# Strassen's method for the up projections of a two-layer decoder trunk

## The chip, the cores and the metric

The kernel runs on one core of one Trainium2 chip. The metric is the time on the device of one execution, in microseconds (us). TensorE (PE in the profile, with PEld for its weight loads) does the matrix products and writes to PSUM; VectorE (DVE), ScalarE (ACT) and GpSimd (POOL) do the elementwise work; the SyncE queue (SP) starts the transfers.

## The reference

The reference is one inference step of a trunk with two layers, for a prompt of 512 tokens and for 8 samples of 8 tokens. The kernel treats these as one matrix of T = 576 tokens. Layer 0 mixes the tokens by attention and a recurrent branch, layer 1 by causal pooling, and each layer ends in a gated network with a short convolution in time:

```python
def _conv_ffn(xn, prev, w_up, cw, cb, w_down):
    u = jnp.einsum("btd,df->btf", xn, w_up)          # 1024 -> 6144
    uc, new_prev = _causal_dwconv(u, prev, cw, cb)   # three taps in time
    g, val = jnp.split(uc, 2, axis=-1)               # 3072 each
    return jnp.einsum("btf,fd->btd", jax.nn.gelu(g) * val, w_down), new_prev
# in _trunk, for each layer, after the mixer:
xn = _rmsnorm(x, p["norm_ffn"][layer])
y, fb = _conv_ffn(xn, ffn_buf[layer], p["ffn_w_up"][layer], ...)
x = x + y
```

Everything is float32. The change touches the two calls of `_conv_ffn` alone.

## The kernel before

The residual lies transposed in `xT`: eight chunks of 128 channels (on partitions) by 576 tokens. Products are made in three parts: each float32 operand is split into a rounded part and a remainder, and rounded times rounded, rounded times remainder and remainder times rounded are added in PSUM. `split` (L115) makes the two parts of 128 weight columns by 1024 rows (tile `whl`): ACT rounds and DVE subtracts. `mm3` (L126) makes one block of 128 output channels: for each of K chunks of the contraction three weight blocks, each used for both halves of the tokens (HT = 288 columns), so 6K matmuls into two PSUM banks.

A gated network is `ffn` (L1216). Its input is `xgh`, `xgl`: the two parts of x times the gain, not yet divided by the root mean square. The division comes after the product. `rstd` (L233) works out the factor while the first products run and spreads it over partitions in `rb`, and the evacuation of every up product multiplies by `rb`. `up_pair(i)` (L1244) makes column block i of the gate half and of the value half. Each is 48 matmuls in `mm3`, three evacuations (L1268 to L1270) into `u`, three taps of the convolution (L1277 on ACT, L1278 and L1279 on DVE, with small copies of state on POOL); then follow the gelu, the product of the halves (L1284, L1285), and its split into `hh`, `hl` (L1288, L1289). After each eight blocks `down(p)` (L1301) multiplies by 1024 rows of the down weights: eight output chunks of 48 matmuls, each added to `xT` by `add_x` (L703). The weights come by transfers of 1 MB for two column blocks (`raw`, L109).

There are 24 blocks, so one gated network has 24 x 96 = 2304 matmuls up and 24 x 48 = 1152 down. PSUM is one pool of eight banks. Small work (`states`, `tails`) hangs in the queue `bg` and is put in by `tick` between products. The order on each engine is the scheduler's of the language, which keeps near to the order of the program; a queue is run in that order.

## Time and profile before

| | us |
|---|---|
| median of three runs | 1289.35 (1287.3 to 1292.38) |
| the profiled execution | 1290.56 |
| its span in the trace | 1288.8 |
| PE busy | 1272.3 (99%) |
| DVE busy | 816.6 (63%) |
| ACT busy | 536.3 (42%) |
| POOL busy | 167.6 (13%) |

The profiled execution is 1.8 us longer than its span and 0.1% above the median. Busy time of PE counts a matmul until its modelled end, so a busy PE says that it never stood empty, not that it was at its peak; the rate is read from the chain of work, which gives so many matmuls in so many us.

### The profile page before, as it was taken

How to read it: one execution, taken by the hardware profiler on the slowest of the kernel's cores; microseconds unless marked ns; L12 is line 12 of the kernel's file. 1: busy time of each engine (PE TensorE's matmuls, PEld its weight loads, DVE VectorE, ACT ScalarE, POOL GpSimd, SP SyncE). 2: the span in 40 equal slices, each digit the busy share in tenths (PEclk: the TensorE clock that was granted, in tenths of full speed). 3: DMA queues.
4: the chain of work that ended last, by engine and by line, in shares of the span. 5: the costliest groups of instructions: out<-in, count | busy, mean ns of one | idle time of the engine just before them, and what ended most of it. 6: DMA issues, size and time to landing. Idle time of an engine off the chain costs nothing.

```text
span 1288.8 us, 22949 instructions
## 1 busy us (share of the span) xinstructions
PE 1272.3 (99%) x9422; PEld 1221.3 (95%) x9422; DVE 816.6 (63%) x1571; ACT 536.3 (42%) x889; POOL 167.6 (13%) x530
## 2 busy tenths in 40 slices
PE   8999989999999999999999999999999999999998
PEld 6988878889999999999999999899999999999998
DVE  6847979887767436664376658766643767346742
ACT  6656567764434213432234336443412343124331
POOL 2240064282100000000000003210000000000000
PEclk9999999999999999999999999999999999999999
DMA  6223343342322232222322112422232232233131
GB/s 167 97 68 102 100 138 89 90 161 69 103 68 76 68 117 81 68 68 86 113 66 65 62 36 74 149 71 67 68 100 99 67 101 68 67 99 100 35 96 47
DMA packets 105918, 111.64 MB, mean 87 GB/s; under 512 B 6722, under 2 KB 96970, under 8 KB 105805
## 3 DMA queue, kind: packets, MB, share of 16 engines
q1 hardware_dynamic: 101668, 101.68, 24.5%
q0 software_dynamic: 3072, 8.46, 2.4%
q8 instruction: 74, 1.21, 0.4%
q14 instruction: 32, 0.25, 0.1%
q10 hardware_dynamic: 1072, 0.04, 0.1%
HBM read 104.14 MB, written 6.25 MB: 86 GB/s over the span
## 4 chain that ended last, share of the span: by engine, by line
PE 78%; DVE 5%; ACT 1%; issue 1%; ACTq 0%
PE mmb L135 73%; PE mmb L903 1%; PE mmb L691 1%; PE mmb L866 1%; DVE whl L123 1%; DVE xl L285 0%; PE mmb L920 0%; ACT zh L1149 0%; DVE eb L836 0%; PE mmb L849 0%; DVE st L833 0%; DVE xT L1179 0%; PE mmb L1232 0%; DVE zl L1150 0%; DVE pl L853 0%
## 5 line engine op out<-in xcount | busy, mean ns | idle before, releaser
L135 PE MATMUL mmb<-xh,whl 128*128 128x288 f32 x3456 | 613.8, 298 | 0.0
L135 PEld LDWEIGHTS mmb<-xh,whl 128*128 128x128 f32 x3456 | 512.2, 189 | 2.7 <-ACT kT L649 0.2
L135 PE MATMUL mmb<-xl,whl 128*128 128x288 f32 x1728 | 371.6, 296 | 1.6 <-DVE xl L285 1.6
L122 ACT CAST whl<-wraw 128x1024 fp32r<-128x1024 f32 (+1 forms) x172 | 178.7, 1040 | 365.2 <-PE mmb L135 261.3
L135 PEld LDWEIGHTS mmb<-xl,whl 128*128 128x128 f32 x1728 | 279.2, 189 | 2.2 <-DVE xl L285 2.1
L135 PE MATMUL mmb<-hh,whl 128*128 128x288 f32 x1536 | 269.8, 295 | 0.1
L123 DVE TENSOR_TENSOR whl<-wraw,whl 128x1024 fp32r<-128x1024 f32 (+1 forms) x172 | 209.8, 1220 | 84.2 <-ACT whl L122 83.9
L135 PEld LDWEIGHTS mmb<-hh,whl 128*128 128x128 f32 x1536 | 225.7, 188 | 0.7 <-ACT hh L1288 0.6
L135 PE MATMUL mmb<-hl,whl 128*128 128x288 f32 x768 | 164.8, 295 | 0.0
L703 DVE TENSOR_TENSOR xT<-mmb,xT 128x288 f32<-128x288 f32 x112 | 46.1, 452 | 146.6 <-PE mmb L135 146.3
L1268 DVE TENSOR_TENSOR u<-mmb,rb 128x288 f32<-128x288 f32 x96 | 44.0, 458 | 134.2 <-PE mmb L135 127.5
L1273 POOL COPY ut<-u 128x18 f32<-128x18 f32 x96 | 23.1, 241 | 777.7 <-DVE u L1270 777.7
L135 PEld LDWEIGHTS mmb<-hl,whl 128*128 128x128 f32 x768 | 122.9, 188 | 0.0
L1288 ACT CAST hh<-hf 128x576 fp32r<-128x576 f32 x48 | 32.4, 674 | 139.0 <-DVE hf L1285 139.0
L1277 ACT ACTIVATE t<-u,par 128x592 f32<-128x592 f32 x96 | 84.7, 882 | 3.6 <-POOL u L1272 2.0
L1279 DVE SCALAR_TENSOR_TENSOR t<-u,par,t 128x592 f32<-128x592 f32 x96 | 80.2, 835 | 3.4
L1278 DVE SCALAR_TENSOR_TENSOR t<-u,par,t 128x592 f32<-128x592 f32 x96 | 79.5, 828 | 1.1 <-ACT t L1277 1.0
L1282 ACT ACTIVATE t<-t 128x592 f32<-128x592 f32 x48 | 33.6, 700 | 94.9 <-DVE t L1279 94.9
L1289 DVE TENSOR_TENSOR hl<-hf,hh 128x576 fp32r<-128x576 f32 x48 | 36.4, 758 | 34.8 <-ACT hh L1288 34.8
L580 PE MATMUL mmb<-whl,xh 128*128 128x512 f32 x192 | 53.2, 394 | 0.0
L580 PEld LDWEIGHTS mmb<-whl,xh 128*128 128x128 f32 x192 | 35.3, 188 | 8.1 <-ACT a__257 L1462 0.4
L1269 DVE TENSOR_TENSOR u<-mmb,rb 128x224 f32<-128x224 f32 x96 | 36.5, 380 | 0.0
(394 smaller groups left out, 1321.7 us busy)
## 6 DMA issues: line engine op xcount, KB each, us to landing
wraw<-in_ffn_w_up SPq DMA_DIRECT2D x48, 1024.0 KB
wraw<-in_ffn_w_down SPq DMA_DIRECT2D x24, 1024.0 KB
wraw<-in_ab_w_in SPq DMA_DIRECT2D x9, 1024.0 KB
wraw<-in_ab_w_out SPq DMA_DIRECT2D x4, 1024.0 KB
xt<-in_x_prompt SPq DMA_DIRECT2D x4, 512.0 KB
out_y_p<-y SPq DMA_DIRECT2D x8, 256.0 KB
wraw<-in_ab_w_in SPq DMA_DIRECT2D x2, 512.0 KB
out_k_p<-X SPq DMA_DIRECT2D x1, 1024.0 KB
```

The source lines that it names most:

```text
L122: keep(self.nc.scalar.copy(hi, v))
L123: keep(self.nc.vector.tensor_tensor(lo, v, hi.bitcast(F32), SUB))
L135: nc.tensor.matmul(ps[hf][:, 0:HT], w[:, k, :], x[:, hf * HT:(hf + 1) * HT], start=(n == 0 and j == 0), stop=(n == K - 1 and j == 2))
L580: PE.matmul(ps[i], x[:, i * P:(i + 1) * P], w[:, k2, :], start=(k == 0 and j == 0), stop=(k == 7 and j == 2))
L703: self.nc.vector.tensor_tensor(x, ps[hf][:, 0:HT], x, ADD)
L1268: V.tensor_tensor(u[:, 2:2 + HT], ps[0][:, 0:HT], self.rb[:, 0:HT], MUL)
L1269: V.tensor_tensor(u[:, 2 + HT:514], ps[1][:, 0:NP - HT], self.rb[:, HT:NP], MUL)
L1277: A.activation(t, u[:, 2:594], AF.Identity, scale=self.fw(l, 2, ch), bias=self.fb(l, ch))
L1278: V.scalar_tensor_tensor(t, u[:, 1:593], self.fw(l, 1, ch), t, MUL, ADD)
L1279: V.scalar_tensor_tensor(t, u[:, 0:592], self.fw(l, 0, ch), t, MUL, ADD)
L1282: A.activation(tg[:, 0:592], tg[:, 0:592], AF.Gelu_apprx_tanh)
L1289: V.tensor_tensor(hl, hf_, hh.bitcast(F32), SUB)
```

## The change

The change makes blocks 0 and 1 of each gated network as before, and the other 22 blocks of each half (44 column blocks, taken in pairs, 22 units) by Strassen's method in Winograd's form. The weights of a unit are cut into four quarters (two column blocks by two halves of the 1024 rows), the input into four (two halves of the channels by two halves of the tokens), and seven products take the place of eight. For that the input has to be the finished normed one: `normed` makes `xn` = x times gain times `rb`, splits its four quarters into `xa`, `xb`, and makes the four sums of quarters on POOL, in place; `sums` splits those sums into the tiles that held `xgh`, `xgl`. In each unit POOL makes four sums of weight quarters (512 elements for each partition), `wform` splits each of the seven weight matrices (512 elements), the products of 12 matmuls add up in three PSUM tags (X and Y with two banks, Z with one), and the evacuations add banks. The down projection is made in six blocks of 512 rows (four chunks of h) in place of three of 1024; the first five blocks' 40 steps of 24 matmuls stand between the products of the units, and the last eight after them, in groups of three, three and two. The weights come by four transfers of 256 KB for each unit, each issued after the last form of the quarter it replaces; three PSUM banks are left for everything else until the last block.

The core of the diff:

```diff
+            def normed():
+                for c in range(4):
+                    for k in (c, c + 4):
+                        V.scalar_tensor_tensor(xn[k], self.xT[:, k, :], self.g_ffn(l, k), self.rb, MUL, MUL)
+                    for x, v in ((xa, xn[c][:, 0:HT]), (xb, xn[c + 4])):
+                        A.copy(x[0][:, c, :], v)
+                        V.tensor_tensor(x[1][:, c, :], v, x[0][:, c, :].bitcast(F32), SUB)
+                    a0, a1 = xn[c][:, 0:HT], xn[c][:, HT:T]
+                    b0, b1 = xn[c + 4][:, 0:HT], xn[c + 4][:, HT:T]
+                    G.tensor_tensor(a0, a1, a0, SUB)
+                    G.tensor_tensor(a1, b1, a1, SUB)
+                    G.tensor_tensor(b1, b1, a0, SUB)
+                    G.tensor_tensor(b0, b0, b1, SUB)
...
+            def sums():
+                for h, (n0, n1) in enumerate((("t1", "t3"), ("t4", "t2"))):
+                    th, tl = self.half("xh", h), self.half("xl", h)
+                    for c in range(4):
+                        v = xn[4 * h + c]
+                        A.copy(th[:, c, :], v)
+                        V.tensor_tensor(tl[:, c, :], v, th[:, c, :].bitcast(F32), SUB)
...
+            def wform(v):
...
+                with self.tc.high_priority():
+                    A.copy(f[:, 0], v)
+                    V.tensor_tensor(f[:, 1], v, f[:, 0].bitcast(F32), SUB)
+                return f
+
+            def prod(ps, w, x, start):
+                for k in range(4):
+                    for j, (a, b) in enumerate(((0, 0), (0, 1), (1, 0))):
+                        PE.matmul(ps[:, 0:HT], w[:, a, k, :], x[b][:, k, :], start=(start and k == 0 and j == 0),
+                                  stop=(k == 3 and j == 2), skip_group_check=True)
...
+                def w1():
+                    G.tensor_tensor(a21, a11, a21, SUB)
...
+                    G.tensor_tensor(d, a22, a21, SUB)
+                    w = wform(a11)
+                    G.tensor_tensor(a11, d, a11, ADD)
+                    return w
+
+                def w2():
+                    w = wform(a12)
+                    G.tensor_tensor(a12, a12, st["d"], SUB)
+                    return w
...
+            put(0, "12")
+            put(1, "1")
+            put(0, "5")
+            for n in range(22):
+                nx = n + 1 if n < 21 else None
+                put(n, "6")
+                if nx is not None and n:
+                    put(nx, "1")
+                if n >= 3:
+                    put_down()
+                put(n, "7")
+                if nx is not None:
+                    put(nx, "25")
+                if n >= 2:
+                    put_down()
+                put(n, "43")
+            while downs:
+                put_down()
...
+            for j, (kind, a, b) in enumerate(plan):
+                prepare(j + 3)
```

Here `V`, `A`, `G` and `PE` are the four engines, and `prepare` makes the weight form of the product three places ahead. The `conv` and `gate` of the changed kernel are the old lines as functions.

The order in three places. First DVE at the start of layer 0's gated network, from the first evacuation of the second up pair on. Before, evacuation, taps, gate and split follow each other:

```order
L1268 TENSOR_TENSOR u<-mmb,rb 128x288
L1269 TENSOR_TENSOR u<-mmb,rb 128x224
L1289 TENSOR_TENSOR hl<-hf,hh 128x576
L1270 TENSOR_TENSOR u<-mmb,rb 128x8x8
L123 TENSOR_TENSOR whl<-wraw,whl 128x1024
```

Now, in the same place:

```order
L1305 TENSOR_TENSOR u<-pu,rb 128x288
L1306 TENSOR_TENSOR u<-pu,rb 128x224
L1275 TENSOR_TENSOR hf<-t 128x512
L1359 TENSOR_TENSOR whl<-wraw,whl 128x512 x2
L1276 TENSOR_TENSOR hf<-t 128x64
L1307 TENSOR_TENSOR u<-pu,rb 128x8x8
L1323 SCALAR_TENSOR_TENSOR xn<-xT,par,rb 128x576
L1280 TENSOR_TENSOR hl<-hf,hh 128x576
L1323 SCALAR_TENSOR_TENSOR xn<-xT,par,rb 128x576
L1326 TENSOR_TENSOR xa<-xn,xa 128x288
L1323 SCALAR_TENSOR_TENSOR xn<-xT,par,rb 128x576
L1326 TENSOR_TENSOR xb<-xn,xb 128x576
```

The eight `xn`, their eight splits and eight weight forms stand between two up pairs and their taps; the eight splits of the sums (L1343) follow later in the queue.

Second, POOL in the same stretch. Before, after the last constants of the pooling layer (`bp`), it had only a memset and two small copies for each column block:

```order
L1085 CAST bp<-bpt 120x64
L1272 COPY u<-fstT 128x8x2 x2
L1271 MEMSET u 128x2
L1272 COPY u<-fstT 128x8x2
L1271 MEMSET u 128x2
L1272 COPY u<-fstT 128x8x2
L1273 COPY ut<-u 128x18 x2
```

Now the sums of the input and of the weights:

```order
L1399 TENSOR_TENSOR wraw<-wraw,d 128x512
L1263 COPY ut<-u 128x18
L1392 TENSOR_TENSOR d<-wraw 128x512
L1329 TENSOR_TENSOR xn<-xn 128x288
L1330 TENSOR_TENSOR xn<-xn 128x288
L1331 TENSOR_TENSOR xn<-xn 128x288
L1332 TENSOR_TENSOR xn<-xn 128x288
L1394 TENSOR_TENSOR wraw<-d,wraw 128x512
```

Each group of four `xn` sums waits for DVE's splits of that chunk, and the splits of the sums wait for POOL.

Third, DVE in the middle of a gated network. Before, one column block:

```order
L1268 TENSOR_TENSOR u<-mmb,rb 128x288
L1269 TENSOR_TENSOR u<-mmb,rb 128x224
L1270 TENSOR_TENSOR u<-mmb,rb 128x8x8
L123 TENSOR_TENSOR whl<-wraw,whl 128x1024
L1278 SCALAR_TENSOR_TENSOR t<-u,par,t 128x592
L1279 SCALAR_TENSOR_TENSOR t<-u,par,t 128x592
L1284 TENSOR_TENSOR hf<-t 128x512
L1285 TENSOR_TENSOR hf<-t 128x64
L1289 TENSOR_TENSOR hl<-hf,hh 128x576
```

Now a part of one unit (`wd` are down weights):

```order
L1268 SCALAR_TENSOR_TENSOR t<-u,par,t 128x592
L1269 SCALAR_TENSOR_TENSOR t<-u,par,t 128x592
L1268 SCALAR_TENSOR_TENSOR t<-u,par,t 128x592
L1359 TENSOR_TENSOR whl<-wd,whl 128x512
L1359 TENSOR_TENSOR whl<-wraw,whl 128x512
L1269 SCALAR_TENSOR_TENSOR t<-u,par,t 128x592
L1275 TENSOR_TENSOR hf<-t 128x512
L1276 TENSOR_TENSOR hf<-t 128x64
L1275 TENSOR_TENSOR hf<-t 128x512
L1276 TENSOR_TENSOR hf<-t 128x64
L711 TENSOR_TENSOR xT<-mmb,xT 128x288
L1280 TENSOR_TENSOR hl<-hf,hh 128x576
```

The weight forms have half the width of before and are three times as many, and the taps of two column blocks come together.

## Rows read from the trace of the kernel before

**Rows 1.** The page's head, its engines and the granted clock of 40 slices.

```profile
span 1288.8 us, 22949 instructions
...
PE 1272.3 (99%) x9422; PEld 1221.3 (95%) x9422; DVE 816.6 (63%) x1571; ACT 536.3 (42%) x889; POOL 167.6 (13%) x530
...
PEclk9999999999999999999999999999999999999999
```

**Rows 2.** The chain that ended last: start us, us, what.

```profile
203.87 1.60 PE mmb L691 x12
...
426.60 95.98 PE mmb L135 x720
```

**Rows 3.** The steady stretch by windows: us, each engine's busy us, clock, DMA.

```profile
400.00:700.00 300.00, 300.00 (x2255) 299.82 (x2254) 170.40 (x279) 95.86 (x118) 11.68 (x93) 1.00 0.25 80
```

**Rows 4.** DVE groups by shape: count, busy us, mean ns, idle before.

```profile
L123 DVE TENSOR_TENSOR whl<-wraw,whl 128x1024 fp32r<-128x1024 f32 x168 | 207.1, 1233 | 84.1 <-ACT whl L122 83.9
L1279 DVE SCALAR_TENSOR_TENSOR t<-u,par,t 128x592 f32<-128x592 f32 x96 | 80.2, 835 | 3.4
L1278 DVE SCALAR_TENSOR_TENSOR t<-u,par,t 128x592 f32<-128x592 f32 x96 | 79.5, 828 | 1.1 <-ACT t L1277 1.0
L703 DVE TENSOR_TENSOR xT<-mmb,xT 128x288 f32<-128x288 f32 x112 | 46.1, 452 | 146.6 <-PE mmb L135 146.3
...
L1269 DVE TENSOR_TENSOR u<-mmb,rb 128x224 f32<-128x224 f32 x96 | 36.5, 380 | 0.0
L1289 DVE TENSOR_TENSOR hl<-hf,hh 128x576 fp32r<-128x576 f32 x48 | 36.4, 758 | 34.8 <-ACT hh L1288 34.8
L1284 DVE TENSOR_TENSOR hf<-t 128x512 f32<-128x512 f32 x48 | 33.2, 692 | 1.8
L1270 DVE TENSOR_TENSOR u<-mmb,rb 128x64 f32<-128x64 f32 x96 | 20.6, 214 | 0.0
...
L1285 DVE TENSOR_TENSOR hf<-t 128x64 f32<-128x64 f32 x48 | 10.5, 218 | 0.0
...
L285 DVE SCALAR_TENSOR_TENSOR xl<-xT,gm,xh 128x576 fp32r<-128x576 f32 x8 | 6.7, 841 | 0.3
...
L123 DVE TENSOR_TENSOR whl<-wraw,whl 128x512 fp32r<-128x512 f32 x4 | 2.8, 690 | 0.0
```

**Rows 5.** ACT by shape: the rounding of 512 weights for each partition.

```profile
L122 ACT CAST whl<-wraw 128x512 fp32r<-128x512 f32 x4 | 2.5, 627 | 10.7 <-issue 10.7
```

**Rows 6.** POOL by shape, then in order of time: a narrow sum, two wide ones.

```profile
L1068 POOL TENSOR_TENSOR bt<-bt,ident 128x128 f32<-128x128 f32 x4 | 1.8, 459 | 0.2
...
811.70 1.43 POOL L295 TENSOR_TENSOR sqacc<-sqacc,sq 128x576 f32<-128x576 f32 x1 [1.09 <-ACT sq L293]
813.60 1.42 POOL L295 TENSOR_TENSOR sqacc<-sqacc,sq 128x576 f32<-128x576 f32 x1 [0.48 <-ACT sq L293]
```

**Rows 7.** DVE in order of time beside those two sums.

```profile
811.15 0.74 DVE L1179 SCALAR_TENSOR_TENSOR xT<-mmb,par,xT 128x512 f32<-128x512 f32 x1
...
812.00 3.63 DVE L285 SCALAR_TENSOR_TENSOR xl<-xT,par,xh 128x576 fp32r<-128x576 f32 x2
```

**Rows 8.** DVE and POOL in order of time after the recurrent branch.

```profile
173.59 2.65 DVE L469 TENSOR_TENSOR xh<-vt,xh 128x512 fp32r<-128x512 f32 x2 [1.80 <-ACT vt L468]
...
173.05 1.08 POOL L895 TENSOR_TENSOR bn<-cbs,cn 64x512 f32<-64x512 f32 x1 [0.60 <-ACT cbs L745]
174.09 1.59 POOL L898 TENSOR_TENSOR bd<-cbs,ds 128x512 f32<-128x512 f32 x1
```

**Rows 9.** Start of layer 0's gated network: first evacuation (DVE), second up pair (chain).

```profile
317.68 0.46 DVE L1268 TENSOR_TENSOR u<-mmb,rb 128x288 f32<-128x288 f32 x1 [2.40 <-ACT rb L257]
...
326.17 6.58 PE mmb L135 x48
```

**Rows 10.** Start of layer 1's gated network: chain, then window with granted clock.

```profile
817.50 6.44 PE mmb L135 x36
...
817.00:820.00 3.00, 3.00 (x18) 2.97 (x18) 2.25 (x9) 0.56 (x1) 0.00 (x0) 0.55 0.00 0
```

**Rows 11.** One us of a 1 MB weight load, as a window.

```profile
316.00:317.00 1.00, 1.00 (x5) 0.24 (x3) 0.00 (x0) 0.00 (x0) 0.00 (x0) 1.00 1.09 388
```

More of the change, by code (lines that the diff above doesn't have):

```diff
@@ new lines, in ffn, with dn_w, dn_p @@
+            ts = {}
+            rd = {}
+            def dn_w(q, m):
+                if m % 2 == 0:
+                    rd[0] = fp.tile([P, 4, 256], F32, name="wd", tag="wd", bufs=2)
+                    nc.sync.dma_start(rd[0], dn[:, q * 4:q * 4 + 4, m * P:(m + 2) * P])
+                return wform(rd[0][:, :, m % 2 * P:m % 2 * P + P])
+            def dn_p(q, m, w, ps=None, ks=range(4)):
+                new = ps is None
+                if new:
+                    ps = self.bank(), self.bank()
+                for k in ks:
+                    for j, (a, b) in enumerate(((0, 0), (0, 1), (1, 0))):
+                        for hf in range(2):
+                            PE.matmul(ps[hf][:, 0:HT], w[:, a, k, :], hs[4 * q + k][b][:, hf * HT:(hf + 1) * HT],
+                                      start=(k == 0 and j == 0), stop=(k == 3 and j == 2))
+                if k == 3:
+                    self.add_x(m, ps)
+                return ps
@@ L1314, in ffn @@
-            for i in range(24):
-                up_pair(i)
-                if i % 4 == 3:
-                    for s in range(2):
-                        self.bg.append(lambda q=i // 4, s=s: tails(q, s))
-                if i % 8 == 0 and i:
-                    down(i // 8 - 1)
-            down(2)
+            self.psum(3)
+            for i in range(2):
+                up_pair(i)
+                if i == 0:
+                    normed()
+            self.up0 = None
+            for n in range(2):
+                for f, h in ((0, 0), (1, 0), (1, 1), (0, 1)):
+                    load(n, f, h)
@@ new lines, in ffn, with put, put_down @@
+            sums()
+            units = {}
+            downs = deque((q, m) for q in range(5) for m in range(8))
+            plan = []
+            def put(n, names):
+                for c in names:
+                    plan.append(("up", n, c))
+            def put_down():
+                plan.append(("down",) + downs.popleft())
+            put(0, "12")
[14 more added lines that the diff above has]
+                put(n, "43")
@@ new lines, in ffn, with prepare @@
+            while downs:
+                put_down()
+            ready = {}
+            def prepare(j):
+                if j < len(plan):
+                    kind, a, b = plan[j]
+                    if kind == "up":
+                        if a not in units:
+                            units[a] = unit(a)
+                        ready[j] = units[a][b][0]()
+                    else:
+                        ready[j] = dn_w(a, b)
+            for j in range(3):
+                prepare(j)
@@ new lines, in ffn @@
+            for j, (kind, a, b) in enumerate(plan):
+                prepare(j + 3)
+                if kind == "up":
+                    units[a][b][1](ready.pop(j))
+                else:
+                    dn_p(a, b, ready.pop(j))
+                if kind == "down" or a < 3:
+                    self.tick()
+            after(None)
+            ms = [range(0, 3), range(3, 6), range(6, 8)]
+            ws = {}
+            for m in range(3):
+                ws[m] = dn_w(5, m)
+            self.psum(8)
@@ new lines, in ffn @@
+            for g in ms:
+                ps = {}
+                for m in g:
+                    ps[m] = dn_p(5, m, ws[m], None, range(2))
+                for m in g:
+                    dn_p(5, m, ws[m], ps[m], range(2, 4))
+                    if m + 3 < 8:
+                        ws[m + 3] = dn_w(5, m + 3)
+                    after(m)
+                    if len(self.bg) > 1:
+                        self.tick()
+                    if self.mid:
+                        self.mid.popleft()()
```

188 lines of the change are left out of this document (142 added, 46 removed).

## The prediction

> **What bounds the kernel now.** I read the page's head first: PE is busy for 1272.3 of 1288.8 us, and its clock is at the full level (2.4 GHz) in all 40 slices [rows 1]. So the time is a number of matmuls times a rate. The rate stands in the chain of waits: 720 matmuls of 288 columns take 95.98 us, 133.3 ns each [rows 2]. It doesn't hang on two matmuls sharing their weights, as they do in `mm3`: 12 matmuls with 12 different weight blocks take 1.60 us, again 133 ns [rows 2]. That matters, since Strassen's products use each weight block once.
>
> Next I asked how much room the other engines have. In a stretch of 300 us in the middle of a gated network DVE is busy for 170.40, ACT for 95.86, POOL for 11.68 us [rows 3]. From the groups by shape one column block costs DVE 3 x 1.233 (splits) + 2 x (0.452 + 0.380 + 0.214) (evacuation, an add of 288 columns for its first part) + 2 x (0.828 + 0.835) (taps) + 0.692 + 0.218 + 0.758 (gate and split) + 2 x 0.452 (`add_x`) = 11.7 us [rows 4]. A column block has 144 matmuls (96 up, 48 down), 19.2 us, so 300 us hold 15.6 of them and the sum is 183; the window shows 170.4. Means overlap at their ends, and below every DVE sum is taken times 0.93.
>
> **What goes.** For each gated network the up products fall from 2304 matmuls to 2 x 96 + 22 x 7 x 12 = 2040; the down products stay at 1152. 264 x 133.3 ns = **35.2 us** per layer, 70.4 in all, if PE stays fed. The rest is about whether it does.
>
> **The middle (units 3 to 21).** A unit has 84 matmuls up and two down steps of 24: 132, 17.6 us of PE. DVE has nine forms of 512 (0.690), one sum of 288 columns (0.452), two of 224 and 64 (0.594), taps for two blocks (3.33), one gate (1.67) and four `add_x` (1.81): 14.7, times 0.93 = 13.7 us [rows 4]. ACT has nine roundings of 0.627 [rows 5], 5.6 us, and four copies of 288 columns at no more than that, 2.5; on top of all its old work (0.32 of 17.6, 5.6 us) that is 13.7, which is still below 17.6. The transfers are 1.5 MB per unit, 89 GB/s, where a load has reached 388 [rows 11]; the quarters in pieces of 512 bytes may be slower, but each has several products of slack.
>
> POOL gets four sums of 512. A sum of 128 columns takes 0.459, one of 576 takes 1.42 [rows 6], so 512 take 1.28 by the line between them (about 1.26 to 1.28; I use 1.26), 5.0 us per unit. Alone that is nothing. But POOL and DVE get in each other's way. While POOL's two sums ran from 811.70 and 813.60, DVE's two instructions with two operands in SBUF, 0.84 us each in the group [rows 4], took 3.63 together: they sat through both sums. The one just before them, which reads PSUM, took its 0.74 [rows 7]. At 173.59 two DVE subtractions of 0.69 took 2.65, with POOL sums of 1.08 and 1.59 around them [rows 8]. So the two engines exclude each other where both read two tiles of SBUF. In a unit of the changed kernel all of DVE's work but the sums from PSUM (3.45 x 0.93 = 3.2 us) is of that kind.
>
> Bounds of a unit on DVE: 13.7 if no two instructions meet, 13.7 + 5.0 = 18.7 if each POOL sum holds DVE for its whole length. PE's 17.6 lies between, nearer the upper end. I take 17.8 as the pace, a fifth of the strict excess, since a collision with an idle or PSUM-reading DVE costs nothing: 19.5 units (one has one down step) x 0.2 = **4 us** per layer (0 to 21).
>
> The Trainium skill has a rule on this ("SBUF — State Buffer", section "Who interferes with whom"): a VectorE instruction with two SBUF inputs contends with a GpSimd instruction that reads SBUF, and the loser is blocked for the whole instruction. It speaks against moving the weight sums to GpSimd. Taken to the letter it makes every unit 18.7 us and is the dear rival below; rows 7 and 8 show such full waits, but not how often they would fall together here.
>
> **Units 0 to 2** have one down step among them, so PE needs only 11.2 us a unit, and DVE 11.5 x 0.93 = 10.7 without and 15.7 with every sum in its way. The upper end is 4.5 x 3 = 13.6 us late; the taps may lag by two units (`u` has two buffers). I take **4** (0 to 14).
>
> **The start** is the dear place. `rb` is there for the first evacuation at 317.68, and the second up pair ends at 326.17 + 6.58 = 332.75 [rows 9]. After it PE has the products 1 and 2 of unit 0 and 1 of unit 1, 36 matmuls, 4.8 us: by 337.5 it wants product 5, whose input is the split of all eight sums of `t1` and `t3`. By the order, DVE has until then, from the first evacuation: 12 evacuations (4.2 us), eight forms (5.5), one old split (1.2), eight taps (6.7), gate and split (1.7), eight `xn` at 0.841 (6.7), four splits of 288 (at 0.45) and four of 576 (at 0.758), 4.8, one sum (0.45) and four splits of sums (3.0): 34.3, times 0.93 = 32.0 us [rows 4]. From 317.7 that ends at 349.7, and PE is 12.2 us late with no lock at all. POOL has in the same time eight weight sums (10.1 us) and 14 of the 16 sums of `xn` at 0.8 (the line of rows 6), 11.1: 21.2. If each holds DVE except beside its PSUM reads (4.3 us), PE is 12.2 + 16.9 = 29 late. Product 6 then needs the other four splits, with 6.3 us of DVE work in the queue before them against 1.6 of PE: 4.7 more, 7.5 with the POOL sums left. Together 17 to 36.5 us. About five weight sums run while DVE waits for the second up pair, so 6.3 of the upper end fall away: I take **30**. It is near the strict end because here both queues are full of instructions of the blocking kind, as in rows 7 and 8.
>
> **Clock.** After the short wait of PE at 815 the clock is 0.55 from 817 to 820, near the lower level of 1.2 GHz, and 36 matmuls take 6.44 us in place of 4.80 [rows 10]: 1.6 us for a restart. I count two per layer, **3.2** (1.6 to 6.4). **The end:** after the last unit PE has one down step (3.2 us) and the first half of three more (4.8), while two taps, gates and splits pass through ACT and DVE, some 8 to 9 us from these rows: **1** (0 to 2).
>
> **Sum** per layer: -35.2 + 30 + 4 + 4 + 3.2 + 1 = +7.0; for two layers +14. On the profiled 1290.56 (0.1% above the median) that is **1305 us**. With all lower ends: -35.2 + 17 + 1.6 = -16.6, twice -33: 1257. With all upper ends: -35.2 + 36.5 + 14 + 21 + 6.4 + 2 = +44.7, twice +89: 1380.
>
> **Rivals.** *Cheap lock.* POOL's sums mostly meet DVE idle or on PSUM, or PE can live on the chunks that come early; then the start is 17 to 22 us, the rest little, and the saving stays: 1257 to 1284, say 1268. For it: DVE alone is at 13.7 of 17.6 us, and products 1 and 2 can begin chunk by chunk. Against it: rows 7 and 8, and that DVE's sum for the start is too long even without POOL. *Paid in full.* DVE with POOL sets the pace of every unit, not just the first: 18.7 for 17.6 us, PE waits in each unit, 1335 to 1380 us. It decides when DVE's share and POOL's sums together pass 17.6 us, so from about four fifths of POOL's time in DVE's way. For it: in-order queues that are nearly full seldom keep up. Against it: collisions need both at once. *A new wait on loads and banks.* A weight form stands in DVE's queue ahead of the last evacuation of the first up pair, and waits for a 256 KB quarter and two POOL sums; X has two banks, both held by that pair. By the rows it holds PE for 1 to 5 us per layer; alone it would leave the gain: 1290.6 - 70.4 + 10 = 1230. The sums above say it isn't alone.
>
> **How the numbers follow.** Likeliest case (start dear, middle nearly fed), 1284 to 1335: 0.49; cheap lock, 1257 to 1284: 0.34; paid in full, over 1335: 0.13; loads and banks alone, below 1257: 0.04. Of the likeliest case 0.13 lies within 0.5% of the time before (1283 to 1296; about what a measurement can tell from no change). So faster 0.38, same 0.13, slower 0.49. The range goes from 1257 to 1335, 0.83; the likeliest case's own is 1284 to 1335.
>
> **What would show it.** The matmul count (9422 before) must fall by 528, and 12 products in the middle must take 1.6 us. Start: PE must have waits of 10 us and more between the second up pair and product 6 of unit 0, ended by DVE's splits, with DVE and POOL busy all the while. Lock: the mean of the DVE forms of 512 must lie well above 0.69 us and that of POOL's sums above 1.28. Middle: windows over whole units must show DVE over 80% and PE nearly full; a PE well below full there means the second rival, forms near 0.69 and a short start the first. I am wrong if PE waits little at the start, or if ACT or a transfer ends its longest waits.

## The result, and where the time went

The changed kernel takes 1322.85 us (median of four runs, 1321.14 to 1323.89), the kernel before 1290.42: the ratio is 1.0252, with an interval of 1.0228 to 1.0277. The forecast was 1305. The sign and the range held, but of the 32.4 us that it got longer the sum had only 14.

The head of the page of the changed kernel, beside [rows 1]:

```profile
span 1321.5 us, 23545 instructions
...
PE 1242.3 (94%) x8894; PEld 1175.5 (89%) x8894; DVE 1050.5 (79%) x1939; ACT 691.3 (52%) x1365; POOL 500.9 (38%) x738
...
PEclk9999999999688999999999999968999999999999
```

The saving is all there: 528 matmuls fewer. But PE is at 94% where it was at 99%, and its clock dips in two places, one per layer. What the new work on DVE and POOL did to one another stands in the groups by shape (count | busy us, mean ns | idle before). DVE first, then POOL, to be read against [rows 4] and [rows 6]:

```profile
L1359 DVE TENSOR_TENSOR whl<-wraw,whl 128x512 fp32r<-128x512 f32 x264 | 210.8, 819 | 20.4 <-ACT whl L1358 17.5
L1268 DVE SCALAR_TENSOR_TENSOR t<-u,par,t 128x592 f32<-128x592 f32 x96 | 99.9, 1042 | 24.6 <-ACT t L1267 24.2
L1359 DVE TENSOR_TENSOR whl<-wd,whl 128x512 fp32r<-128x512 f32 x96 | 65.0, 684 | 7.4 <-ACT whl L1358 7.4
L1280 DVE TENSOR_TENSOR hl<-hf,hh 128x576 fp32r<-128x576 f32 x48 | 51.7, 1081 | 0.0
L1323 DVE SCALAR_TENSOR_TENSOR xn<-xT,par,rb 128x576 f32<-128x576 f32 x16 | 21.7, 1374 | 0.0
...
L1399 POOL TENSOR_TENSOR wraw<-wraw,d 128x512 f32<-128x512 f32 x44 | 67.8, 1542 | 42.7 <-DVE whl L1359 42.6
L1392 POOL TENSOR_TENSOR d<-wraw 128x512 f32<-128x512 f32 x44 | 62.8, 1427 | 33.5 <-DMA wraw<-in_ffn_w_up 20.8 <-DVE whl L1359 10.9 <-POOL u L1262 0.4
L1330 POOL TENSOR_TENSOR xn<-xn 128x288 f32<-128x288 f32 x8 | 9.3, 1162 | 0.5
```

The forms made from raw weights stand beside POOL's sums and take 0.819 us; those from down weights, two thirds of which don't, still take 0.684. Of the 264 forms from raw weights 99 ran beside a sum of POOL, with a mean of 1.04 us, and 165 did not, with 0.684. A tap went from 0.828 to 1.042, the last split of a gate from 0.758 to 1.081. POOL's sums of 512, taken as 1.26, are 1.43 to 1.54; those of 288, taken as 0.8, are 1.16.

**A ledger by stage.** I cut each gated network into a start (117 us from its first up product: the direct pairs, the normed input, units 0 to 2), a middle, and an end (from some 8 us before the last product of unit 21). The kernel before is cut to the same lengths, to within 1.2 us at layer 0's end. The windows show length, then busy time of PE, PEld, DVE, ACT, POOL, the granted clock, the transfers' share and GB/s. The kernel before, layer 0 then layer 1:

```profile
303.40:420.40 117.00, 117.00 (x860) 113.70 (x860) 81.44 (x146) 49.66 (x74) 9.56 (x52) 1.00 0.24 78
420.40:728.00 307.60, 307.53 (x2309) 307.16 (x2307) 175.10 (x287) 98.53 (x121) 11.57 (x90) 1.00 0.25 80
728.00:773.00 45.00, 45.00 (x339) 44.99 (x339) 22.99 (x34) 16.10 (x23) 0.00 (x0) 1.00 0.15 47
807.60:924.60 117.00, 115.38 (x830) 111.67 (x830) 80.52 (x140) 46.18 (x70) 15.04 (x57) 0.99 0.31 98
924.60:1232.30 307.70, 307.70 (x2318) 307.58 (x2317) 175.97 (x290) 98.76 (x120) 12.64 (x90) 1.00 0.24 78
1232.30:1288.80 56.50, 51.61 (x394) 50.76 (x392) 15.23 (x25) 13.31 (x25) 0.00 (x0) 1.00 0.26 78
```

The changed kernel:

```profile
305.60:422.60 117.00, 95.00 (x568) 86.03 (x567) 92.23 (x140) 55.10 (x106) 57.82 (x68) 0.82 0.21 60
422.60:744.10 321.50, 318.34 (x2398) 317.28 (x2397) 273.34 (x454) 167.33 (x316) 131.53 (x177) 1.00 0.29 86
744.10:787.90 43.80, 38.90 (x280) 38.44 (x279) 29.88 (x57) 18.59 (x31) 0.43 (x2) 0.96 0.16 49
823.80:940.80 117.00, 94.86 (x539) 85.37 (x539) 89.97 (x135) 50.81 (x100) 59.59 (x71) 0.80 0.24 68
940.80:1265.00 324.20, 320.81 (x2419) 319.73 (x2418) 275.94 (x457) 168.91 (x319) 131.88 (x178) 1.00 0.29 85
1265.00:1321.50 56.50, 45.01 (x322) 42.70 (x320) 22.64 (x47) 15.71 (x34) 0.43 (x2) 0.95 0.25 72
```

In each window I counted the matmuls of 288 columns (from the groups by shape; one or two at each edge are uncertain) and took off 0.1333 us for each, the full rate of [rows 2]. What is left, the excess, is idle time, slow clock and small matmuls:

| excess, us | layer 0 before | after | layer 1 before | after |
|---|---|---|---|---|
| start | 7.5 (821 matmuls) | 46.3 (530) | 10.6 (798) | 49.4 (507) |
| middle | 0.8 (2301) | 2.8 (2390) | -0.3 (2310) | 2.7 (2411) |
| end | -0.1 (338) | 6.6 (279) | 9.6 (352) | 19.2 (280) |

So per layer the start costs 38.8, the middle 2.0 and 3.0, the end 6.7 and 9.6 us more, against 35.2 saved: 12.3 and 16.1. These make 28.4 of the 32.7 us between the two spans. The rest lies mostly outside the change: 2.2 us ahead of layer 0's network (it began between 304.4 and 310.6 us in the changed kernels run here) and about 1.3 between the networks.

**The start**, by windows of 5 us in layer 0 and three idle times of PE:

```profile
340.00:345.00 5.00, 3.78 (x12) 2.63 (x11) 5.00 (x5) 3.02 (x7) 4.76 (x5) 0.50 0.03 8
350.00:355.00 5.00, 2.01 (x6) 1.25 (x6) 3.18 (x4) 2.31 (x7) 4.45 (x5) 0.50 0.01 4
355.00:360.00 5.00, 4.96 (x20) 4.22 (x20) 4.69 (x6) 2.43 (x5) 4.77 (x5) 0.50 0.05 15
...
352.99 0.85 PE L1365 MATMUL pX<-xa,whl 128*128 128x288 f32 x2 [3.76 <-ACT xa L1325]
373.89 0.61 PE L1365 MATMUL pX<-xl,whl 128*128 128x288 f32 x1 [2.49 <-DVE xl L1343]
401.91 0.43 PE L1503 MATMUL mmb<-ident,ut 128*72 128x128 f32 x1 [3.75 <-POOL ut L1263]
```

POOL is nearly full and DVE too, except in the second window. PE waits for the normed input chunk by chunk, and all the while its granted clock is 0.50, the level of 1.2 GHz. From 355 to 360 it is busy all the time and makes 14 matmuls of 288 columns and 6 small transposes, where 37 such matmuls would fit.

The longest wait there, 3.76 us, ends with a copy on ACT. ACT in order of time:

```profile
349.40 0.67 ACT L1342 CAST xh<-xn 128x576 fp32r<-128x576 f32 x1 [3.58 <-POOL xn L1330]
351.93 0.67 ACT L1342 CAST xh<-xn 128x576 fp32r<-128x576 f32 x1 [1.75 <-POOL xn L1332]
352.51 0.43 ACT L1325 CAST xa<-xn 128x288 fp32r<-128x288 f32 x1
```

The chunk that `xa` copies was ready on DVE at 348.71. The copy stood in ACT's queue behind two roundings of sums (`xh`), and these waited for POOL.

The third idle time has nothing to do with the normed input. A small transpose of the convolution's state (`tails`, L1503) stands between products of units 2 and 3, and it waited for POOL's copy of 18 columns of `ut`:

```profile
399.43 1.80 POOL L1399 TENSOR_TENSOR wraw<-wraw,d 128x512 f32<-128x512 f32 x1
401.18 0.68 POOL L1263 COPY ut<-u 128x18 f32<-128x18 f32 x1
```

The copy's input was ready on DVE at 398.14, but it stood behind two sums of weights that ran from 398.20 on. From 401.9 to 408 the clock was 0.53, and the next 24 matmuls took 5.62 us in place of 3.20. In layer 1 the same wait is 3.10 us.

**The end**, layer 0. PE, then DVE, in order of time:

```profile
751.80 0.56 PE L1365 MATMUL pY<-xb,whl 128*128 128x288 f32 x3
...
762.40 0.70 PE L1495 MATMUL mmb<-hh,whl 128*128 128x288 f32 x2 [3.75 <-DVE xT L711]
...
759.46 0.68 DVE L1275 TENSOR_TENSOR hf<-t 128x512 f32<-128x512 f32 x1
760.06 0.22 DVE L1276 TENSOR_TENSOR hf<-t 128x64 f32<-128x64 f32 x1
760.19 0.45 DVE L711 TENSOR_TENSOR xT<-mmb,xT 128x288 f32<-128x288 f32 x1
760.56 1.42 DVE L1280 TENSOR_TENSOR hl<-hf,hh 128x576 fp32r<-128x576 f32 x2
761.90 0.45 DVE L711 TENSOR_TENSOR xT<-mmb,xT 128x288 f32<-128x288 f32 x1
```

The last product of unit 21 ends at 752.2. PE then makes the down step that is left, whose 24 matmuls end near 755.5, and the first 12 of the last block. The next output has to wait for a bank, that is, for the `add_x` (L711) of that step; on DVE it stands behind taps and gates of both last blocks and runs at 760.19 and 761.90. Of the 36 matmuls that were to cover the gate, 24 come only after it. Before that PE had waited 1.14 us for a bank that a copy of `tails` (L1505) held, and from 763 to 766 the clock was 0.50. In layer 1 the same two waits are 3.76 and 1.15 us.

### The profile page after: what moved, and what is told of

Same layout as the page of the kernel before. It is cut to its first block, busy times and chain, and to the rows that moved or that the text cites. A ratio compares the mean times of both kernels' runs of the same rounds, so it can differ in the third digit from the quotient of the medians.

```text
span 1321.5 us, 23545 instructions
## 1 busy us (share of the span) xinstructions
PE 1242.3 (94%) x8894; PEld 1175.5 (89%) x8894; DVE 1050.5 (79%) x1939; ACT 691.3 (52%) x1365; POOL 500.9 (38%) x738
## 3 DMA queue, kind: packets, MB, share of 16 engines
q8 instruction: 70, 1.15, 0.4%
## 4 chain that ended last, share of the span: by engine, by line
PE 70%; DVE 16%; ACT 4%; POOL 3%; issue 3%; DMA 2%; SPq 0%; ACTq 0%; DVEq 0%; POOLq 0%
PE mmb L1495 19%; PE pX L1365 18%; PE pY L1365 9%; PE mmb L143 6%; PE mmb L588 5%; PE pZ L1365 4%; DVE whl L1359 4%; DVE t L1268 2%; PE pu L143 2%; DVE hl L1280 1%; PE mmb L911 1%; DVE t L1269 1%; ACT whl L1358 1%; DVE hf L1275 1%; DMA wraw<-in_ffn_w_up 1%
## 5 line engine op out<-in xcount | busy, mean ns | idle before, releaser
L1365 PE MATMUL pX<-xh,whl 128*128 128x288 f32 x1056 | 240.3, 303 | 3.7 <-ACT c L1450 2.7
L1359 DVE TENSOR_TENSOR whl<-wraw,whl 128x512 fp32r<-128x512 f32 x264 | 210.8, 819 | 20.4 <-ACT whl L1358 17.5
L1358 ACT CAST whl<-wraw 128x512 fp32r<-128x512 f32 x264 | 156.9, 619 | 93.3 <-PE mmb L1495 51.6
L1365 PEld LDWEIGHTS pX<-xh,whl 128*128 128x128 f32 x1056 | 182.1, 194 | 5.6 <-ACT c L1450 3.6
L1365 PE MATMUL pX<-xl,whl 128*128 128x288 f32 x528 | 159.4, 302 | 5.3 <-DVE xl L1343 5.3
L711 DVE TENSOR_TENSOR xT<-mmb,xT 128x288 f32<-128x288 f32 x208 | 87.0, 449 | 69.9 <-PE mmb L1495 68.1
L1263 POOL COPY ut<-u 128x18 f32<-128x18 f32 x96 | 36.5, 380 | 259.2 <-DVE u L1427 257.5
L1365 PE MATMUL pX<-xa,whl 128*128 128x288 f32 x528 | 90.4, 318 | 18.9 <-ACT xa L1325 10.2
L1365 PEld LDWEIGHTS pX<-xl,whl 128*128 128x128 f32 x528 | 102.2, 194 | 6.5 <-DVE xl L1343 6.5
L1365 PEld LDWEIGHTS pX<-xa,whl 128*128 128x128 f32 x528 | 80.4, 205 | 22.6 <-ACT xa L1325 11.9
L1365 PE MATMUL pZ<-xb,whl 128*128 128x288 f32 x528 | 86.4, 309 | 1.6 <-ACT whl L1358 1.3
L1365 PE MATMUL pY<-xb,whl 128*128 128x288 f32 x528 | 78.7, 298 | 0.0
```

Of the source, the lines that this page charges most:

```text
L711: self.nc.vector.tensor_tensor(x, ps[hf][:, 0:HT], x, ADD)
L1358: A.copy(f[:, 0], v)
L1359: V.tensor_tensor(f[:, 1], v, f[:, 0].bitcast(F32), SUB)
L1365: PE.matmul(ps[:, 0:HT], w[:, a, k, :], x[b][:, k, :], start=(start and k == 0 and j == 0), stop=(k == 3 and j == 2), skip_group_check=True)
```

## Experiments

Ratios are to the kernel before, run on the same chip; the changed kernel is at 1.0252.

**1. More work held back for the end.**

```diff
-                if n >= 3:
+                if 3 <= n < 20:
                     put_down()
```

> Two down steps of each layer are held back from units 20 and 21 and run after unit 21, ahead of the last block; nothing is left out. Changed kernel: 1322.9 us. Theory (the end is uncovered): after the last product of unit 21 the gate chain takes some 10 us, TensorE has 36 matmuls (4.8 us) for it, and then runs at a lower clock; two more steps of 24 matmuls (6.4 us) fill the hole. Units 20 and 21 then hold 14.4 us of TensorE work each, above VectorE's 13.4. Expected 7.5 excess in layer 0 and about 9 in layer 1 go down by 4 to 7 each: 1309 to 1315. Rival (the switch to eight banks sets the hole, since it waits for the same evacuations whatever stands ahead of it): within 3 us of 1322.9. Rival (the middle has no slack, VectorE sets its pace): units 20 and 21 lose what the end wins, 1318 to 1324.

Measured 1.0206 (1.0185 to 1.0228), 1319.69 us, some 6 us less than the changed kernel. The excess of the end fell from 6.6 to 4.0 and from 19.2 to 15.5, that of the start stayed at 47.3 and 47.7. So the cover was short, and units 20 and 21 had room to give it up. But 2.6 and 3.7 are less than the 4 to 7 expected: PE still waits 1.9 us for L711 and 1.3 for a copy of `tails` (L1505) at layer 0's end. Both theories own a part of it, the thin cover and the wait for banks. The time alone lies in the band of the third, a middle without slack, but the middle's excess rose by only 0.3 and 0.6.

**2. The sums of the normed input on VectorE**, all four of a chunk.

```diff
-                    G.tensor_tensor(a0, a1, a0, SUB)
+                    V.tensor_tensor(a0, a1, a0, SUB)
...
```

> The 16 sums of the normed input (four a chunk, L1330 to L1333) run on VectorE instead of GpSimd, the rest as it is; nothing is left out. Theory (at the start GpSimd's 1.16 us sums and VectorE's stretched forms beside them set the pace): 18.6 us of GpSimd per layer become 16 x 0.45 = 7 us of VectorE, and the 8 products with the scale go from 1.37 back to 0.9; the start gets 5 to 12 us shorter per layer, 1298 to 1313. Rival (VectorE's own total sets the start, GpSimd's sums run beside it for little): 7 us more on VectorE per layer less some 4 that are no longer stretched, 1322 to 1332.

Measured 1.0195 (1.0173 to 1.0217), 1320.01 us. The start's excess fell by 1.4 and 3.2 only (44.9, 46.2). The chain of waits had shown POOL's four sums a chunk one behind the other, 1.2 us each; they went, and DVE's 16 sums came in their place. The gain is real, but below the 5 to 12 us per layer expected; the rival expected none. At this place both engines are full, and work moved from one to the other stays in the way.

**3. No normed input at all.** `stand` gives the seven products the old halves.

```diff
-                if i == 0:
-                    normed()
...
-            sums()
+            stand()
```

> Left out: the normed input and its sums (L1320 to L1347 whole); the seven products read the old halves in their place, so the values are another network's. Weight sums, forms, evacuations, downs stay. Theory (the normed input without cover is most of the start's 39 us over TensorE's own time): 25 to 32 us per layer go, 1259 to 1273. Rival (the weight sums on GpSimd and the few downs of units 0 to 2 are most of it): 5 to 10 us per layer go, 1303 to 1313.

Measured 0.9805 (0.9781 to 0.9829), 1270.05 us, 0.0447 of the time before or 58 us less than the changed kernel. The start's excess is 20.1 and 21.0, so the normed input costs 26.2 and 28.4 us per layer. What remains over the kernel before, 12.6 and 10.4, belongs to units 0 to 2; 3.0 and 3.4 of it are PE's wait for the transpose of `ut`. The first theory holds.

**4. Four direct blocks instead of two.**

```diff
-            for i in range(2):
+            for i in range(4):
                 up_pair(i)
                 if i == 0:
                     normed()
...
-            for n in range(22):
+            for n in range(20):
```

> Four column blocks by the old direct products instead of two, units from block 4 on (20 units per layer), downs from unit 0 on; the normed input is made after the first block, its sums' halves overwrite the old ones behind the last direct block. Nothing is left out. The method's gain falls by 24 matmuls, 3.2 us, per layer. Theory (the start lacks cover): 25.6 us more of direct products, of whose time VectorE is free for about a third, hide the normed input and GpSimd's sums; units 0 to 2 have downs. The start's 39 fall to 12 to 18 per layer: 1275 to 1290. Rival (the halves can only be written behind the last direct product, and the gates of blocks 2 and 3 wait for them, so the wait is only moved): 1312 to 1330.

Measured 1.0066 (1.0047 to 1.0085), 1301.97 us: 24 us back, against 6.4 of products given up, though short of the 1275 to 1290 expected. The start's excess is 30.5 and 35.0. The window from 330 to 355 us has PE busy for 14.96 of 25 us at a clock of 0.73: the whole normed input stood in DVE's queue ahead of the evacuations and splits of the next direct block (PE waits 3.6 us for the evacuation L1305 and 3.8 for a copy of convolution state on ACT, L1241). The traced run, at 1295.18 us, was the fastest of five, so its excess is if anything too small.

**5. Fillers for TensorE's idle time.**

```diff
                 for k in range(4):
+                    for _ in range(12 if made[0] <= 6 else 3 if made[0] <= 14 else 0):
+                        PE.matmul(ps[:, 384:512], self.identb, self.identb, start=True, stop=True, ...)
```

> The changed kernel with idle-time fillers: ahead of each of the four chunks of the first six products of a layer stand twelve 128-column matmuls of constants into unread columns of the same bank, ahead of the next eight products three; nothing is left out, 384 small matmuls a layer are added. In the changed kernel (1.0252 of before) TensorE ran at a granted clock of 0.50 from 340 to 365 us, and of the start's 39 us per layer over before's 22 are idle time and 17 are matmuls at the lower clock. Theory (the low clock is a cost of its own): the fillers lie in the idle time, the clock stays at 1.0 and 8 to 17 us per layer come back, ratio 1.000 to 1.014. Rival (VectorE and GpSimd set the start, and what the clock gives back turns into idle time): within 3 us per layer, ratio 1.020 to 1.030, the idle share larger, the clock near 1.0.

Measured 1.0348 (1.0316 to 1.038), 1341.73 us. (The fillers begin sums of their own in the products' banks, so these products are not the network's.) The windows of the start:

```profile
340.00:350.00 10.00, 6.20 (x50) 5.04 (x49) 10.00 (x10) 5.71 (x11) 8.70 (x8) 0.74 0.02 6
350.00:360.00 10.00, 6.55 (x49) 5.82 (x50) 8.18 (x8) 2.83 (x7) 8.89 (x8) 0.67 0.10 30
370.00:380.00 10.00, 10.00 (x127) 9.03 (x125) 9.16 (x15) 2.46 (x8) 0.45 (x1) 1.00 0.11 33
```

The clock rose (0.74 and 0.67 where it was 0.50, 1.00 from 370 on) and PE's idle time in the start fell from 22.0 to 11.9 us, but the excess, which counts the fillers too, rose to 50.9 and 53.1. The fillers that met no idle time stood in the way of products, and the waits for DVE didn't go. So a better clock alone brought nothing here; what it would bring without the fillers' own time this run can't tell.

**6. The weight sums on VectorE.** The four sums of `w1` and `w2` are issued on V at high priority, the rest is as it was.

```diff
-                    G.tensor_tensor(a21, a11, a21, SUB)
-                    G.tensor_tensor(d, a22, a21, SUB)
+                    with self.tc.high_priority():
+                        V.tensor_tensor(a21, a11, a21, SUB)
+                        V.tensor_tensor(d, a22, a21, SUB)
```

> The four weight sums of each unit (L1390 to L1399) run on VectorE instead of GpSimd; nothing is left out. GpSimd's 5.9 us per unit become some 4 x 0.7 = 2.8 us on VectorE, and VectorE's operations beside them go back from 0.82 to 0.69 (forms) and from 1.04 to 0.83 (taps). Theory (the middle is fed by TensorE, its price is independent of the stretching): the middle stays at 17.8 us per unit within 0.1; the start gets 0 to 8 us shorter per layer, since the sums of units 0 to 2 are no longer 1.5 us each: ratio 1.012 to 1.026. Rival (VectorE is at 85% in the middle and the stretching is what costs): with the stretching gone the middle gets faster by 0.2 us or more per unit, 9 us in all, with the start together below 1.010; or, if VectorE is too full for 2.8 us more, the units get longer, over 1.030.

Measured 1.0055 (1.0035 to 1.0076), 1302.69 us: 25 us less, more than expected. The start's excess is 37.5 in both layers (8.8 and 11.9 less), the middle's 1.5 and 1.1 (1.3 and 1.6 less). Head of the page and DVE's groups:

```profile
PE 1234.7 (95%) x8894; PEld 1168.2 (90%) x8894; DVE 1055.5 (81%) x2115; ACT 691.0 (53%) x1365; POOL 273.3 (21%) x562
...
L1359 DVE TENSOR_TENSOR whl<-wraw,whl 128x512 fp32r<-128x512 f32 x264 | 176.7, 686 | 11.4 <-ACT whl L1358 8.8
L1268 DVE SCALAR_TENSOR_TENSOR t<-u,par,t 128x592 f32<-128x592 f32 x96 | 77.5, 841 | 7.2 <-ACT t L1267 7.2
L1280 DVE TENSOR_TENSOR hl<-hf,hh 128x576 fp32r<-128x576 f32 x48 | 35.5, 750 | 0.1
L1392 DVE TENSOR_TENSOR wraw<-wraw 128x512 f32<-128x512 f32 x44 | 31.5, 715 | 9.2 <-DMA wraw<-in_ffn_w_up 8.8
```

DVE took over 176 sums, 121.8 us of work, and its busy time rose by 5.0 us, from 1050.5 to 1055.5: the forms are back at 0.686, the taps at 0.841, the splits at 0.750. POOL's 227.6 us had bought nothing. The time is near the rival's, but the place is the first theory's: the middle gained 3 us in all, and most came back at the start. The largest wait that went is that of the transpose of `ut`: 3.75 and 3.10 us in the changed kernel, 0.3 and 0.2 here, where POOL has no weight sums for the copy to stand behind. From 390 us to the start's end the clock is 1.00. With the slow matmuls behind it, that wait is some 6 of the 8.8 us in layer 0 (an estimate: 3.5 of idle time and 2.4 of slow clock). How much of the rest comes from sums of 0.7 us in place of 1.5 ahead of the forms, this run doesn't part.

**7. The normed input spread over the direct blocks.** As in 4, with one chunk after block 0, one after block 1, two after block 2, the sums' halves behind block 3, and four down steps held for the end.

```diff
-                    normed()
+                normed(((0,), (1,), (2, 3), ())[i])
```

> The run with four direct blocks (1.0066 of before), with the normed input made a chunk after block 0, one after block 1 and two after block 2 instead of four after block 0, its halves behind block 3, and four down steps held for the end instead of two. Nothing is left out. Theory (the splits of the direct blocks queued behind the whole of the normed input on VectorE, 10 us idle and a clock of 0.73 from 330 to 355): 6 to 12 us per layer come back at the start and 2 to 4 at the end, ratio 0.985 to 0.997. Rival (VectorE's work is only moved to behind block 3, where TensorE then waits for it): 1.000 to 1.010.

Measured 0.9896 (0.9872 to 0.9921), 1281.57 us: faster than the kernel before. The start's excess is 24.3 and 25.0, which gives back the 6 to 12 us expected there. The end's is 3.1 and 15.2, only 1.7 and 0.2 less than in 4, where 2 to 4 were expected. PE is busy throughout from 330 to 365 us, and what is left comes behind block 3:

```profile
330.00:350.00 20.00, 20.00 (x147) 19.31 (x146) 19.52 (x31) 10.17 (x16) 10.45 (x13) 1.00 0.17 56
...
365.00:380.00 15.00, 9.14 (x35) 7.40 (x35) 14.37 (x16) 7.28 (x15) 12.39 (x13) 0.62 0.08 23
```

**8. The same with fillers.**

```diff
+                    for _ in range(6 if made[0] <= 6 else 3 if made[0] <= 14 else 0):
+                        PE.matmul(ps[:, 384:512], self.identb, self.identb, start=True, stop=True, ...)
```

> The run before this one with fillers as in the other run with fillers, six ahead of each chunk of a layer's first six products by the method, three ahead of the next eight. If the low clock is a cost of its own there too, 2 to 6 us per layer below the run without them; if the waits take over, the same within 3 us or longer by up to 5.

Measured 1.0093 (1.0061 to 1.0124), 1305.96 us, 24 us slower than without (the products are changed as in 5). The start's excess rose to 37.8 and 39.3. That is worse than both expectations. As in 5, the fillers cost more than they give.

**9. Experiment 7 with the weight sums on VectorE.** The edits of 7 and of 6, for instance

```diff
-                    G.tensor_tensor(a12, a12, st["d"], SUB)
+                    with self.tc.high_priority():
+                        V.tensor_tensor(a12, a12, st["d"], SUB)
```

> The run with four direct blocks and the spread normed input (0.9896 of before), with the weight sums on VectorE as in the run that moved them (which took the changed kernel from 1.0252 to 1.0055). Nothing is left out. If GpSimd's sums of 1.5 us hold up units 0 to 2 here too (24 us per layer over TensorE's own time are left at the start), 3 to 8 us per layer come back there and 1.5 in the middle: ratio 0.975 to 0.983. Rival (the start is now VectorE's own total, and four more operations per unit there stand in the way of the direct blocks' splits): 0.988 to 0.996.

Measured 0.9862 (0.984 to 0.9884), 1273.19 us. The start's excess is 23.4 and 22.9, the middle's 2.5 and 2.0. That is a gain of 0.0034 of the time over 7, between the two bands, and the intervals overlap: with downs from unit 0 on and a fuller DVE, the move brings little more at the start.

**10. Both kinds of sums on VectorE in the changed kernel.** The edits of 2 and 6 together:

```diff
-                    G.tensor_tensor(b0, b0, b1, SUB)
+                    V.tensor_tensor(b0, b0, b1, SUB)
...
-                    G.tensor_tensor(a11, d, a11, ADD)
+                    with self.tc.high_priority():
+                        V.tensor_tensor(a11, d, a11, ADD)
```

> The changed kernel with both kinds of sums, of the normed input and of the weights, on VectorE; nothing is left out. Alone, the first took 1.0252 to 1.0195, the second to 1.0055. If the two returns are of the same cause, VectorE's and GpSimd's operations stretching each other, and separate in place, they add: 0.998 to 1.003. If VectorE's own total is what is left at the start, the 7 us of sums of the normed input weigh and it stays at 1.003 to 1.012.

Measured 1.0006 (0.9991 to 1.0021), 1291.57 us. The two returns add (0.0057 and 0.0197 off 1.0252 is 0.9998). Taking POOL's sums away gives back as much as the change had lost; the method's saving then just pays for the rest. DVE's products with the scale now take 0.807 us in place of 1.374. The start still has an excess of 34.3 and 36.7.

**11. The down projection's part alone.** All 24 column blocks by `up_pair`, down steps of 512 rows in between, one left for the end; no products by the method.

```diff
+            for i in range(24):
+                up_pair(i)
+                for _ in range((2, 3, 3 if i < 22 else 2, 0)[i % 4] if i > 3 else 0):
+                    q, m = downs.popleft()
+                    dn_p(q, m, dn_w(q, m))
```

> One part of the change alone: all 24 column blocks by the old direct products, the down projection in blocks of 512 rows in between as in the changed kernel, one step left for the end, the last block's eight outputs behind the switch to eight banks. No products by the method, no normed input, no weight sums; nothing is left out, as many matmuls as before. Theory (the end belongs to the blocks of 512 rows: the last gate has too little behind it): the end's 7 to 10 us per layer appear here by themselves, less what a single block's gate is shorter than two's, 4 to 8 per layer, and nothing elsewhere: ratio 1.005 to 1.012. Rival (the end belongs to the units, whose last two gates come together): 0.998 to 1.003. Rival (the order in the middle costs too, forms made twice as often): over 1.015.

Measured 1.0135 (1.011 to 1.016), 1309.87 us, between the first and the last expectation. By stage, layer 0 and layer 1:

```profile
421.70:736.10 314.40, 313.98 (x2334) 310.54 (x2333) 187.98 (x341) 101.75 (x138) 13.38 (x94) 1.00 0.26 82
736.10:781.10 45.00, 43.51 (x324) 42.84 (x323) 31.07 (x57) 17.71 (x28) 0.82 (x2) 1.00 0.15 48
...
933.90:1252.40 318.50, 317.35 (x2376) 313.84 (x2375) 192.82 (x349) 103.56 (x140) 14.76 (x97) 1.00 0.26 83
1252.40:1308.90 56.50, 47.91 (x343) 45.58 (x341) 20.12 (x41) 14.23 (x30) 0.82 (x2) 0.94 0.19 53
```

Against the kernel before the end has 2.0 us more in layer 0 (1.9 for -0.1) and 6.8 in layer 1 (16.4 for 9.6), the start about 1, and the middle 3.5 and 3.1 (4.3 for 0.8, 2.8 for -0.3). So in layer 0 most of the changed kernel's 6.7 is the units', whose two last gates come together. In layer 1 the down blocks by themselves lose 6.8 of 9.6; but the changed kernel has the same two waits in both layers, so how the 9.6 divides is not shown. The 3 us in the middle, with PE hardly idle, I had not expected. The waits of the weight loads show where most of them lie (PEld; us in total, times, longest; layer 0):

```profile
PEld mmb L1464 <- DVE xT L711: 2.2, 10, 0.6
```

Ten times in a layer a weight load of a down step waited for the `add_x` of an earlier step, that is, for a bank: 2.2 us in layer 0 and 3.0 in layer 1. Only three banks are left for the down steps here, as in the changed kernel. No run with more banks tests this.

**12. Experiment 9 with the sums of the normed input on VectorE too.** The edits of 7, 6 and 2 together:

```diff
-                    G.tensor_tensor(a1, b1, a1, SUB)
+                    V.tensor_tensor(a1, b1, a1, SUB)
```

> The run with four direct blocks, the spread normed input and the weight sums on VectorE (0.9862 of before), with the sums of the normed input on VectorE as well; nothing is left out. In the changed kernel that step took 1.0055 to 1.0006 once the weight sums were on VectorE. If the two engines' stretching each other still costs at the start (23 us per layer over TensorE's own time are left there, some 15 over before), 1 to 3 us per layer come back: 0.980 to 0.985. Rival (VectorE, nearly full in the direct blocks, sets the start, and 7 us more of sums there are 7 us more): 0.987 to 0.997.

Measured 0.9854 (0.9836 to 0.9873), 1272.18 us, the same as 9; the start's excess is 22.2 and 22.7. It lies between the two bands, at the edge of the first. With four direct blocks POOL's sums no longer matter; 12 to 15 us per layer over the kernel before's start remain, behind the last direct block, where the halves of the sums overwrite the old input. In layer 1, 3.7 us of them are again the transpose that waits for `ut`, now late on DVE's evacuation and not on a sum. 9 and 12 beat both kernels.

## Why the prediction was right in sign and too small

- **What bounds the kernel, the saving and the rate**: right. The matmul count fell by 528, and in the middle 12 products in a row take 1.6 us:

```profile
749.17 1.61 PE pX L1365 x12
```

- **The start, 30 us** (17 to 36.5): right, 26.2 and 28.4 by taking the normed input away (experiment 3). The size was that of the sum near the strict end. Its make-up was not as told, though. I had idle time, and of the start's 38.8 us only 22.0 and 20.5 are more idle time than before (117.00 less 95.00, and 115.38 less 94.86). I had POOL holding DVE; on the chain POOL's sums stand by themselves, and they reached PE through ACT's queue as well. With all of them on VectorE (experiment 10) the start keeps an excess of 34.3 and 36.7. So the good number is in part luck. A sign that I had named as showing me wrong came up too: ACT ended the longest wait, 3.76 us in layer 0 and 4.2 in layer 1.
- **Units 0 to 2 and the clock, 4 and 3.2 us**: too small together, 12.6 and 10.4. The sum for the units counted how much of POOL's time falls in DVE's way. It had no term for POOL's small copies, which stand behind its sums: the longest wait there is the transpose of `ut`, 3.75 and 3.10 us and a slow clock after it, and it went when the sums left POOL (experiment 6). The clock was taken as two restarts of 1.6 us [rows 10]. In fact it stood at 0.50 from 340 to 365 us, and 45 matmuls of 288 columns and 12 small transposes took 17.39 us of PE, where the 45 at the full rate take 6.0. Of the start's 38.8 us, 16.8 and 18.3 are not idle time but a busy PE below the full rate. On the chain of waits only some 6 (layer 0) and 12 us (layer 1) are matmul time over 133 ns; the rest of the slowness ran beside DVE's and POOL's work. So the slow clock is partly a price and partly a mark of the waits, and experiment 5 didn't part the two.

The stretch from 340 us, as one window:

```profile
340.00:365.00 25.00, 17.39 (x57) 13.00 (x57) 22.32 (x24) 13.53 (x30) 23.32 (x23) 0.50 0.09 28
```

- **The middle, 4 us** (pace 17.8): right in size, 2.0 and 3.0, with PE at 99% and DVE at 85%. But no unit runs at a slower pace. All of PE's idle time there, 3.2 us in layer 0 and 3.4 in layer 1, is four waits, each of a down block's first step for the split of its last gate (us in total, times, longest; layer 0):

```profile
PE mmb L1495 <- DVE hl L1280: 3.2, 4, 0.8
```

Experiment 6 took 1.3 and 1.6 us away and left one wait a layer, of 1.4 and 1.5 us, so about half of it goes with POOL's sums. The Trainium skill ("SBUF — State Buffer", section "Who interferes with whom") says that the losing instruction is blocked for the whole of the other. The forms' 0.819 against 0.686 agree that DVE is held up; taken for every sum it made 18.7 us a unit, and the middle measured denies that.
- **The end, 1 us** (0 to 2): this is the step that failed. It measured 6.7 and 9.6, some 14 us more, of 18 that were missing in all. (Units and clock add some 9 more; the start and the middle were taken some 8 too dear, and 3.5 lie outside the stages.) I set 3.2 + 4.8 us of matmuls against 8 to 9 us of gates. The gates ended 10 us after the last product, and of the 4.8 only 1.6 could run, since the next output waited for a bank whose `add_x` stood behind the gates in DVE's queue. I had named what hides the gate, but not what the cover itself waits for. The new order of the down blocks, which I had put at nothing, loses 2.0 us in layer 0 and 6.8 in layer 1 by itself (experiment 11).
- **Rivals.** "Cheap lock" fell: its start of 17 to 22 us was not there. "Paid in full" fell in the middle; units 0 to 2 came near its size, but in good part by the wait for `ut`. "Loads and banks" showed, though not alone: the third pair's product waits 0.90 us for L1307, and on layer 1's chain a load of a weight quarter stands with 3.26 us, at 892.80.
- The forecast for the likeliest case, 1284 to 1335, held the time.

## What to carry to other kernels

Before a sum goes to GpSimd, price it in VectorE's time: here 176 sums on VectorE made it busy for only 5 us more than with all of them on GpSimd. And look for what will stand behind it in the queue: a copy of 18 columns, wanted by a small transpose, cost TensorE 3.75 us. Work that must be done before a faster method can begin wants matmuls beside it that don't need it: two more blocks by the old method, with the preparation spread between them and a longer cover at the end, cost 6.4 us of products and gave 46 net. And of each piece of cover, ask whether its own banks and buffers are free at that moment, not only whether it is long enough.

## What the runs showed of the hardware

- VectorE's operations with two operands in SBUF took 0.819 (forms), 1.042 (taps) and 1.374 us (products with the scale) on the mean in the kernel with GpSimd's sums, and 0.686, 0.841 (both experiment 6) and 0.807 (experiment 10) without. The Trainium skill ("Perfetto Trace Analysis", section "Optimizing Scalar/DVE Operations") says that moving work between the two might not help. Moved back to VectorE the sums helped by 2%. The means above agree with its reason, a read port of SBUF that the two share, but part of the 2% is the wait for `ut`, which comes from GpSimd's queue.
- PE's clock stayed at 0.50 from 340 to 365 us, with PE busy for 17.39 of the 25 us and for 4.96 of the 5 from 355. It rose as products followed each other from 366 on (0.83 from 365 to 370), and was at 0.50 again from 375 to 380, after 5 us in which PE had been busy for 1.90.
- A busy PE can hide waits: in experiment 11's middle it stood empty for 0.4 of 314 us, while its weight loads waited 2.2 us for banks, and the stretch took 3.5 us more than before for its matmuls.
